# Pinning the loads, additions and stores of precomputed weight sums in their queues, and dealing the jobs out anew

## The chip, the cores and the metric

The kernel runs on one core of one Trainium2 chip. The metric is the device time of one execution in microseconds (us); the median of three runs stands for a kernel. A profile is taken of one further execution. The engines are called PE (matrix products; PEld is its weight load), DVE (elementwise work and sums), ACT (copies, activations, and the issue of stores), POOL, and SP (the issue of loads). Each works through its own queue in order.

## The reference

Two residual layers over 256 tokens of width 2048 in float32: layer 0 mixes tokens with neighbourhood attention, layer 1 with a gated short convolution; after each comes a gated MLP of width 5632 with a convolution of three taps.

```python
def reference(...):
    h = x
    for i in range(DEPTH):                       # DEPTH = 2
        a = rms_norm(h, mix_norm[i])
        if m == 0:
            mixed = neighborhood_attention(a, na_w_qkv[j], na_rpb[j], na_w_o[j])   # 16 heads of 128
        elif m == 1:
            mixed = short_conv_mixer(a, sc_w_in[j], sc_conv_w[j], sc_w_out[j])     # W_out(B * conv3(C * h))
        h = h + mixed
        h = h + conv_glu_ffn(rms_norm(h, ffn_norm[i]), ffn_w_up[i], ffn_conv_w[i], ffn_conv_b[i], ffn_w_down[i])
    return rms_norm(h, final_norm)
```

## The kernel before, in words

Each float32 factor is split into two parts, hi and lo, and a product is made of three matrix products of such parts (hi by hi, hi by lo, lo by hi). The activations are split once and stay in SBUF. The weights stream from HBM in chunks of up to 512 KB: a load into a `raw` buffer (SP, lines 140, 145, 147; 6 buffers), a copy to `hi` on ACT (L171), and `lo = raw - hi` on DVE (L172; 6 buffers of each).

The program is a list of stages, each a row of items that PE takes in turn:

- `Phase` (L259, L267): the result stands with features on the partitions. A chunk is 128 output features by 8 tiles of the inner dimension; an item is mostly two feature tiles, 4 chunks. The query and key projections (`wqk`, four phases of 8 feature tiles, called QK0 to QK3 here), the up projections (`wup`, 44 feature tiles each, UP0 to UP3) and the input of the convolution (`wsc`, 48 feature tiles, SC) are phases.
- `Values` (L660 to L662): the value projection of four heads, 8 chunks and 8 items; one stands behind each QK phase (V0 to V3). Attention of those heads runs between: after a head's key come its scores (L590 to L592) two ticks later, its probabilities (L615) four ticks later, and the mix with the values after the value products.
- `Tokens` (L454 to L456): the result stands with tokens on the partitions and is added to the residual `h` (L347). These are the output of attention (`wo`), the four down projections (`wdown`; first and third by one plan, second and fourth by another, called DOWN0 to DOWN3) and the output of the convolution (`wscout`, OUT). Each has two groups of 1024 output columns. Some pairs of inner tiles are computed with seven products instead of eight, which needs sums of weight blocks. In pairs marked S, DVE makes the sums from the raw weights on the spot (lines 180 to 184). In pairs marked D they are read from DRAM, where a job left them earlier (the tile `kept`).

A job (`make`) is one half of the sums of one D pair: two loads of 256 KB into two `act` tiles (L198, on SP), four additions of 128x256 on DVE (L204 to L207), and two stores of 256 KB issued by ACT (L211). There are 76. They are listed in the order in which the Tokens stages need them, and a table deals them out to the phases: `QK_JOBS` for QK0 to QK3, `UP_JOBS` for UP0 to UP3, `SC_JOBS` for SC. Within a phase the jobs are entered in the list of chunks from an eighth of the items on to three quarters. When a chunk is prepared, the job's loads are recorded; its additions are recorded four entries of the chunk list later, its stores seven entries later. `act` tiles (22 buffers) also hold the inputs of the Tokens stages.

What sets the order: the program records its instructions in this order, and a scheduler then places them on the engines' queues by what it takes to be ready, so that an instruction recorded later can stand ahead of one recorded earlier where neither needs the other. `tc.issue_after(x)` forbids that for one pair of instructions of the same engine: what is recorded inside it stands behind `x`. It sets no bound the other way: the instruction can still slip back. Before the change it is used for a few places (the norm factor, the residual), and not for the jobs.

## Time and profile before

| what | value |
|---|---|
| median of three runs | 2233.21 us (2231.29 to 2233.58) |
| profiled execution, its own time | 2233.43 us |
| span of the profiled execution (first to last instruction) | 2231.6 us |
| granted TensorE clock, mean | 0.996 |
| PE busy | 2194.1 us (98%) |
| DVE busy | 1836.9 us (82%) |
| ACT busy | 1298.0 us (58%) |
| DMA | 530.67 MB, mean 238 GB/s |

PE's records run over one another (the matmuls are pipelined and their ends are modelled), so the 98% don't say how close PE is to its peak. What a stage could take is seen better from the distance between equal products in a stretch without waits, and from stages of equal content against one another. The time between the end of the span and the profiled execution's own time is 1.8 us.

The stages by time (us from the start of the span), as the lines of the products change: QK0 5.6, V0 57.8, QK1 81.8, V1 135.1, QK2 162.5, V2 214.8, QK3 242.4, V3 292.8, `wo` 316.3, UP0 405.4, DOWN0 652.3, UP1 763.8, DOWN1 1008.3, SC 1132.3, OUT 1410.2, UP2 1499.4, DOWN2 1746.3, UP3 1857.9, DOWN3 2102.4.

### The profile page before, as it was taken

How to read it: one execution, taken by the hardware profiler on the slowest of the kernel's cores; microseconds unless marked ns; L12 is line 12 of the kernel's file. 1: busy time of each engine (PE TensorE's matmuls, PEld its weight loads, DVE VectorE, ACT ScalarE, POOL GpSimd, SP SyncE). 2: the span in 40 equal slices, each digit the busy share in tenths (PEclk: the TensorE clock that was granted, in tenths of full speed). 3: DMA queues.
4: the chain of work that ended last, by engine and by line, in shares of the span. 5: the costliest groups of instructions: out<-in, count | busy, mean ns of one | idle time of the engine just before them, and what ended most of it. 6: DMA issues, size and time to landing. Idle time of an engine off the chain costs nothing.

```text
span 2231.6 us, 33123 instructions
## 1 busy us (share of the span) xinstructions
PE 2194.1 (98%) x11728; PEld 1893.3 (85%) x11728; DVE 1836.9 (82%) x2960; ACT 1298.0 (58%) x1967; POOL 102.4 (5%) x143
## 2 busy tenths in 40 slices
PE   9999999999999999999999999999999999999998
PEld 8878888888888888888788888878888888888886
DVE  8787679888888788878897788798888888887887
ACT  7554555666655656566564445566666655666565
POOL 0021110000000000000000001000000000000000
PEclk9999999999999999999999999999999999999999
DMA  8688656677657877767899997776776687665585
GB/s 279 224 291 280 197 173 219 205 237 234 213 177 255 273 233 245 245 197 248 255 304 325 319 337 248 249 246 199 243 234 195 208 265 245 204 212 190 166 267 174
DMA packets 288790, 530.67 MB, mean 238 GB/s; under 512 B 19568, under 2 KB 187632, under 8 KB 288624
## 3 DMA queue, kind: packets, MB, share of 16 engines
q1 hardware_dynamic: 265360, 488.07, 67.0%
q10 hardware_dynamic: 23264, 40.49, 4.9%
q8 instruction: 92, 1.51, 0.3%
q14 instruction: 74, 0.61, 0.1%
HBM read 486.54 MB, written 41.94 MB: 237 GB/s over the span
## 4 chain that ended last, share of the span: by engine, by line
PE 80%; DMA 9%; DVE 7%; issue 2%; ACT 1%; SPq 0%; ACTq 0%; POOL 0%; DVEq 0%
PE mm L259 36%; PE mm L267 19%; PE mm L454 5%; PE mm L455 5%; PE mm L456 5%; DMA act<-in_wdown 3%; DVE lo L172 3%; DMA raw<-in_wsc 2%; PE mu L454 2%; PE mu L456 2%; PE mu L455 2%; DMA raw<-in_wdown 1%; PE mm L660 1%; PE mm L662 1%; PE mm L661 1%
## 5 line engine op out<-in xcount | busy, mean ns | idle before, releaser
L171 ACT CAST hi<-raw 128x1024 fp32r<-128x1024 f32 (+1 forms) x912 | 908.9, 1013 | 390.6 <-PE mm L456 94.2
L172 DVE TENSOR_TENSOR lo<-raw,hi 128x1024 fp32r<-128x1024 f32 (+1 forms) x852 | 1013.0, 1209 | 128.3 <-ACT hi L171 71.8
L259 PE MATMUL mm<-a,hi 128*128 128x512 f32 x4096 | 961.2, 390 | 1.6 <-DVE h L347 0.8
L259 PEld LDWEIGHTS mm<-a,hi 128*128 128x128 f32 x4096 | 759.3, 188 | 154.5 <-issue 1.2
L267 PEld LDWEIGHTS mm<-a,lo 128*128 128x128 f32 x4096 | 513.5, 191 | 19.8 <-DVE lo L172 7.6
L267 PE MATMUL mm<-a,lo 128*128 128x256 f32 x4096 | 521.3, 283 | 5.3 <-DVE lo L172 5.3
L454 PE MATMUL mm<-hi,act 128*128 128x512 f32 x656 | 256.8, 392 | 2.6 <-DVE h L347 2.5
L456 PE MATMUL mm<-hi,act 128*128 128x512 f32 x656 | 256.0, 390 | 0.0
L455 PE MATMUL mm<-lo,act 128*128 128x512 f32 x600 | 234.4, 391 | 1.3 <-DVE lo L172 1.3
L312 ACT COPY corr<-mm 128x256 f32<-128x256 f32 x256 | 93.9, 371 | 228.1 <-PE mm L267 182.3
L328 DVE SCALAR_TENSOR_TENSOR conv<-pad,pt,conv 128x256 f32<-128x256 f32 x384 | 183.7, 479 | 26.4 <-ACT conv L326 20.7
L326 ACT ACTIVATE conv<-pad,pt 128x256 f32<-128x256 f32 x176 | 105.7, 601 | 149.4 <-DVE pad L318 149.2
L454 PEld LDWEIGHTS mm<-hi,act 128*128 128x128 f32 x656 | 123.7, 189 | 29.1 <-issue 2.8
L456 PEld LDWEIGHTS mm<-hi,act 128*128 128x128 f32 x656 | 123.5, 188 | 25.8
L455 PEld LDWEIGHTS mm<-lo,act 128*128 128x128 f32 x600 | 113.3, 189 | 25.6 <-DVE lo L172 2.5
L313 DVE TENSOR_TENSOR corr<-mm,corr 128x256 f32<-128x256 f32 x256 | 106.3, 415 | 7.9 <-ACT corr L312 7.8
L292 DVE TENSOR_TENSOR act<-conv,act 128x256 fp32r<-128x256 f32 x88 | 37.4, 425 | 72.1 <-ACT act L291 71.9
L318 DVE TENSOR_TENSOR pad<-corr,rstd 128x256 f32<-128x256 f32 x176 | 73.4, 418 | 0.0
L455 PE MATMUL mu<-lo,sf 128*128 128x512 f32 x168 | 67.0, 399 | 5.8 <-DVE lo L172 5.7
L204 DVE TENSOR_TENSOR act<-act 128x256 f32<-128x256 f32 x76 | 31.4, 420 | 45.9 <-DMA act<-in_wdown 34.2
L454 PE MATMUL mu<-hi,sf 128*128 128x512 f32 x168 | 66.0, 393 | 0.3 <-ACT hi L171 0.3
L456 PE MATMUL mu<-hi,sf 128*128 128x512 f32 x168 | 66.1, 394 | 0.0
(158 smaller groups left out, 1548.5 us busy)
## 6 DMA issues: line engine op xcount, KB each, us to landing
raw<-in_wup SPq DMA_DIRECT2D x352, 512.0 KB, 5.0
raw<-in_wdown SPq DMA_DIRECT2D x144, 512.0 KB, 5.3
raw<-in_wsc SPq DMA_DIRECT2D x96, 512.0 KB, 5.9
kept<-act ACTq DMA_DIRECT2D x152, 256.0 KB, 4.8
raw<-kept SPq DMA_DIRECT2D x76, 512.0 KB, 4.9
act<-in_wdown SPq DMA_DIRECT2D x128, 256.0 KB, 6.0
raw<-in_wqk SPq DMA_DIRECT2D x56, 512.0 KB, 5.1
raw<-in_wv SPq DMA_DIRECT2D x32, 512.0 KB, 4.8
```

Of the source, the lines that this page charges most:

```text
L171: nc.scalar.copy(out=hv, in_=r)
L172: nc.vector.tensor_sub(out=lv, in0=r, in1=hv.bitcast(F32))
L259: nc.tensor.matmul(self.ps[ft], lhsT=prepped[i][0][:, o:o + P], rhs=self.src[k], start=k == 0, stop=False)
L267: nc.tensor.matmul(self.ps[ft][:, S:], lhsT=prepped[i][1][:, o:o + P], rhs=self.src[k][:, :S], start=False, stop=k == self.nk - 1)
L312: nc.scalar.copy(out=corr, in_=ps[:, S:])
L313: nc.vector.tensor_add(out=corr, in0=ps[:, :S], in1=corr)
L318: nc.vector.tensor_mul(out=dst, in0=both(ps), in1=rstd)
L326: nc.scalar.activation(c, x[:, 1:S + 1], AF.Identity, scale=w[1], bias=b)
L328: nc.vector.scalar_tensor_tensor(out=c, in0=x[:, tap:tap + S], scalar=w[tap], in1=c, op0=ALU.mult, op1=ALU.add)
L454: nc.tensor.matmul(ps, lhsT=xh, rhs=wh, start=start, stop=False)
L455: nc.tensor.matmul(ps, lhsT=xh, rhs=wl, start=False, stop=False)
L456: nc.tensor.matmul(ps, lhsT=xl, rhs=wh, start=False, stop=stop)
```

## The change

Two things change. First, each load of a job is recorded behind the newest weight load on SP, each addition behind the newest L172 on DVE, and each store behind the newest L171 on ACT; `newest` keeps these three instructions. Second, the jobs are dealt out otherwise: six of the first 16 go to V0, V1 and V2 (entered after the third and, where there are two, the fifth chunk), and SC gives 14 of its 34 to the up projections.

```diff
-QK_JOBS, UP_JOBS, SC_JOBS = (0, 8, 8, 0), (8, 8, 8, 4), 34
+QK_JOBS, V_JOBS, UP_JOBS, SC_JOBS = (0, 4, 4, 2), (2, 2, 2, 0), (10, 10, 12, 8), 20
...
-                nc.sync.dma_start(out=raw[:, :w], in_=src)
+                newest["SP"] = nc.sync.dma_start(out=raw[:, :w], in_=src)
...
-        nc.scalar.copy(out=hv, in_=r)
-        nc.vector.tensor_sub(out=lv, in0=r, in1=hv.bitcast(F32))
+        newest["ACT"] = nc.scalar.copy(out=hv, in_=r)
+        newest["DVE"] = nc.vector.tensor_sub(out=lv, in0=r, in1=hv.bitcast(F32))
...
-            nc.sync.dma_start(out=x.rearrange("p (f n) -> p f n", f=2),
-                              in_=w[f:f + 2, :, 2 * i * P:(2 * i + 2) * P].rearrange("f p n -> p f n"))
+            with tc.issue_after(newest["SP"].ins):
+                nc.sync.dma_start(out=x.rearrange("p (f n) -> p f n", f=2),
+                                  in_=w[f:f + 2, :, 2 * i * P:(2 * i + 2) * P].rearrange("f p n -> p f n"))
...
             add = nc.vector.tensor_add
-            add(out=l[:, 0], in0=l[:, 0], in1=r[:, 0])
...
+            with tc.issue_after(newest["DVE"].ins):
+                add(out=l[:, 0], in0=l[:, 0], in1=r[:, 0])
...
             for n, x in enumerate(tiles):
-                nc.scalar.dma_start(out=dst[:, n, half], in_=x)
+                with tc.issue_after(newest["ACT"].ins):
+                    nc.scalar.dma_start(out=dst[:, n, half], in_=x)
...
-        def __init__(self, g, src):
+        def __init__(self, g, src, jobs=()):
...
                 chunks.append((wv[g, :, k0 * 4 * P:(k0 + 2) * 4 * P], 8 * P, "rows"))
+                if k0 in (4, 8)[:len(jobs)]:
+                    chunks.append((*jobs[k0 // 8], "make"))
...
-        Values(g, a0)
+        Values(g, a0, take(V_JOBS[g]))
```

With all 76 jobs taken, the table before gives UP3 the last two, though it names four. The new table names 76.

What this moves, engine by engine. PE's queue holds the same products in the same order, but for a few that stand some places apart. On SP, at the end of DOWN1, before the change, the loads of five jobs of SC (`act<-in_wscout`) stand among the weight loads of DOWN1 (`raw<-in_wdown`, `raw<-kept`):

```order
L147 DMA raw<-in_wdown 128x4x256 x2
L198 DMA act<-in_wscout 128x2x256 x2
L147 DMA raw<-in_wdown 128x4x256
L198 DMA act<-in_wscout 128x2x256
L147 DMA raw<-in_wdown 128x4x128
L198 DMA act<-in_wscout 128x2x256
L145 DMA raw<-kept_8495 128x1024
L198 DMA act<-in_wscout 128x2x256 x5
L145 DMA raw<-kept_8495 128x1024
L147 DMA raw<-in_wdown 128x4x256 x2
```

In the changed kernel (whose line numbers are up to 5 higher) the end of that stretch, through to the first jobs behind it:

```order
L147 DMA raw<-in_wdown 128x4x256
L147 DMA raw<-in_wdown 128x4x128
L145 DMA raw<-kept_8769 128x1024 x2
L147 DMA raw<-in_wdown 128x4x256 x4
L140 DMA raw<-in_wsc 128x1024 x4
L199 DMA act<-in_wscout 128x2x256 x4
L140 DMA raw<-in_wsc 128x1024
L199 DMA act<-in_wscout 128x2x256 x2
```

The job loads have moved out of DOWN1; the first stand behind the fourth chunk of SC. At the head of OUT the same holds for two jobs, whose loads now stand behind the fourth and fifth chunk of UP2; and two jobs that stood in `wo` now stand at the head of UP0.

On SP in the middle of SC, before (a pair of `act<-` loads is one job):

```order
L198 DMA act<-in_wdown 128x2x256 x4
L140 DMA raw<-in_wsc 128x1024 x5
L198 DMA act<-in_wdown 128x2x256 x6
L140 DMA raw<-in_wsc 128x1024 x8
L198 DMA act<-in_wdown 128x2x256 x4
L140 DMA raw<-in_wsc 128x1024 x5
L198 DMA act<-in_wdown 128x2x256 x8
L140 DMA raw<-in_wsc 128x1024 x6
```

and now:

```order
L199 DMA act<-in_wdown 128x2x256 x4
L140 DMA raw<-in_wsc 128x1024 x7
L199 DMA act<-in_wdown 128x2x256 x4
L140 DMA raw<-in_wsc 128x1024 x5
L199 DMA act<-in_wdown 128x2x256 x4
L140 DMA raw<-in_wsc 128x1024 x7
L199 DMA act<-in_wdown 128x2x256 x2
L140 DMA raw<-in_wsc 128x1024 x5
```

The bunches of two to four jobs have become bunches of one or two, with as many chunks between them.

On DVE at the head of SC, before. `a` is the normalized input of SC, `m`, `z`, `rcol` and `conv` here are steps of the norm's factor, and the additions of a job are `act<-act`:

```order
L172 TENSOR_TENSOR lo<-raw,hi 128x1024
L300 SCALAR_TENSOR_TENSOR a<-tr,pt,a 128x256 x2
L334 TENSOR_SCALAR z<-z 128x2
L172 TENSOR_TENSOR lo<-raw,hi 128x1024
L300 SCALAR_TENSOR_TENSOR a<-tr,pt,a 128x256 x2
L172 TENSOR_TENSOR lo<-raw,hi 128x1024
L300 SCALAR_TENSOR_TENSOR a<-tr,pt,a 128x256 x2
L340 RECIPROCAL m<-m 128x2
L206 TENSOR_TENSOR act<-act 128x2x128
L341 TENSOR_TENSOR m<-m 128x2
L172 TENSOR_TENSOR lo<-raw,hi 128x1024
L300 SCALAR_TENSOR_TENSOR a<-tr,pt,a 128x256
```

and now:

```order
L206 TENSOR_TENSOR act<-act 128x2x128
L337 TENSOR_SCALAR z<-z 128x2
L207 TENSOR_TENSOR act<-act 128x2x128
L172 TENSOR_TENSOR lo<-raw,hi 128x1024
L303 SCALAR_TENSOR_TENSOR a<-tr,pt,a 128x256 x2
L208 TENSOR_TENSOR act<-act 128x2x128
L343 RECIPROCAL m<-m 128x2
L206 TENSOR_TENSOR act<-act 128x2x128
L344 TENSOR_TENSOR m<-m 128x2
L209 TENSOR_TENSOR act<-act 128x2x128
L345 SCALAR_TENSOR_TENSOR m<-m,z 128x2
L207 TENSOR_TENSOR act<-act 128x2x128
```

Eight additions of two jobs stand between the pieces of the input and of the norm's factor where one stood, and two of the L172 that stood ahead of the last piece of `a` have moved behind it.

On DVE at the border from QK1 to V1, before (`qk` and `s` are steps of a head's scores and probabilities):

```order
L605 TENSOR_SCALAR s<-s,z 128x256 x2
L292 TENSOR_TENSOR qk<-qk 128x256
L207 TENSOR_TENSOR act<-act 128x2x128 x2
L204 TENSOR_TENSOR act<-act 128x2x128
L172 TENSOR_TENSOR lo<-raw,hi 128x1024
L205 TENSOR_TENSOR act<-act 128x2x128
L172 TENSOR_TENSOR lo<-raw,hi 128x1024
L206 TENSOR_TENSOR act<-act 128x2x128
L172 TENSOR_TENSOR lo<-raw,hi 128x1024
L207 TENSOR_TENSOR act<-act 128x2x128
L313 TENSOR_TENSOR corr<-mm,corr 128x256
L292 TENSOR_TENSOR act<-tr,act 128x256
```

and now, at the same border:

```order
L172 TENSOR_TENSOR lo<-raw,hi 128x1024 x2
L606 RECIPROCAL z<-z 128x2
L295 TENSOR_TENSOR qk<-qk 128x256
L608 TENSOR_SCALAR s<-s,z 128x256 x2
L206 TENSOR_TENSOR act<-act 128x2x128
L207 TENSOR_TENSOR act<-act 128x2x128
L208 TENSOR_TENSOR act<-act 128x2x128
L209 TENSOR_TENSOR act<-act 128x2x128
L172 TENSOR_TENSOR lo<-raw,hi 128x1024 x2
L316 TENSOR_TENSOR corr<-mm,corr 128x256
L295 TENSOR_TENSOR act<-tr,act 128x256
L571 TENSOR_TENSOR qk<-corr,rstd 128x256
```

Where the additions of two jobs ran into each other and into the L172 of the value products, those of one job stand in a row; the next two jobs stand farther on, among the L172 of V1 and QK2.

More of the change, by code (lines that the diff above doesn't have):

```diff
@@ L144, in prep_to @@
             if kind == "kept":
-                nc.sync.dma_start(out=raw, in_=src().rearrange("p h n -> p (h n)"))
+                newest["SP"] = nc.sync.dma_start(out=raw, in_=src().rearrange("p h n -> p (h n)"))
             else:
-                nc.sync.dma_start(out=raw[:, :4 * w].rearrange("p (f c) -> p f c", f=4),
-                                  in_=src.rearrange("f p c -> p f c"))
+                newest["SP"] = nc.sync.dma_start(out=raw[:, :4 * w].rearrange("p (f c) -> p f c", f=4),
+                                                 in_=src.rearrange("f p c -> p f c"))
             r = raw[:, :4 * w].rearrange("p (f k c) -> p f k c", f=4, c=P)
@@ L185, in sums @@
         return w22, parts(t13), parts(r)
-    kept = {}
+    kept, newest = {}, {}
     def make(job, half):
@@ L203, in adds @@
             add = nc.vector.tensor_add
[L204 to L207 removed]
+            with tc.issue_after(newest["DVE"].ins):
+                add(out=l[:, 0], in0=l[:, 0], in1=r[:, 0])
+                add(out=r[:, 0], in0=r[:, 1], in1=r[:, 0])
+                add(out=r[:, 1], in0=l[:, 0], in1=r[:, 1])
+                add(out=l[:, 1], in0=r[:, 1], in1=l[:, 1])
         def store():
             for n, x in enumerate(tiles):
[L211 removed]
+                with tc.issue_after(newest["ACT"].ins):
+                    nc.scalar.dma_start(out=dst[:, n, half], in_=x)
         stores.append((len(prepped) + 4, adds))
```

3 lines of the change are left out of this document (removed).

## The prediction

> **What bounds the kernel now.** First the page's totals, then the chain of waits for the pace of a stretch without waits, then the busy times by stage, then the waits inside the stages that are too long.
>
> ```profile
> span 2231.6 us, 33123 instructions
> PE 2194.1 (98%) x11728; PEld 1893.3 (85%) x11728; DVE 1836.9 (82%) x2960; ACT 1298.0 (58%) x1967; POOL 102.4 (5%) x143
> 430.19 7.28 PE mm L259 x32
> 437.47 3.83 PE mm L267 x32
> ```
>
> PE is never without work for long, and the chain shows its pace: two feature tiles of a phase take 7.28 us for the long products and 3.83 for the short ones, 11.11 in all; a long product 0.23, a short one 0.12. PE's products are the floor. What can be won is the time that a stage takes beyond them. The stages (length; busy time and instructions of each engine; clock; DMA share; GB/s), in the order V0, QK1, V1, QK2, V2, QK3, V3, UP0, DOWN0, UP1, DOWN1, SC, OUT, UP3 (UP2 is as UP0 to 0.1 us):
>
> ```profile
> 57.80:81.80 24.00, 24.00 (x117) 19.93 (x115) 20.90 (x35) 12.35 (x24) 3.16 (x3) 1.00 0.72 228
> 81.80:135.10 53.30, 51.37 (x311) 45.80 (x310) 38.53 (x81) 25.07 (x45) 5.50 (x2) 1.00 0.80 270
> 135.10:162.50 27.40, 24.28 (x112) 19.55 (x111) 23.59 (x40) 15.08 (x28) 5.85 (x2) 1.00 0.82 273
> 162.50:214.80 52.30, 50.97 (x307) 45.40 (x306) 37.70 (x79) 24.63 (x43) 5.69 (x2) 1.00 0.80 273
> 214.80:242.40 27.60, 24.31 (x113) 19.57 (x112) 23.75 (x40) 15.12 (x28) 4.88 (x2) 1.00 0.83 275
> 242.40:292.80 50.40, 50.40 (x307) 45.28 (x306) 34.00 (x58) 28.36 (x49) 2.04 (x2) 1.00 0.51 163
> 292.80:316.30 23.50, 23.50 (x113) 19.59 (x112) 18.32 (x31) 11.88 (x23) 0.00 (x0) 1.00 0.56 180
> 405.40:652.30 246.90, 246.90 (x1428) 218.59 (x1427) 203.50 (x356) 153.43 (x243) 12.20 (x24) 1.00 0.67 215
> 652.30:763.80 111.50, 111.50 (x494) 92.34 (x493) 92.51 (x107) 66.80 (x74) 0.00 (x0) 1.00 0.77 251
> 763.80:1008.30 244.50, 244.50 (x1409) 216.56 (x1409) 207.32 (x355) 145.83 (x228) 12.30 (x24) 1.00 0.70 228
> 1008.30:1132.30 124.00, 117.18 (x511) 94.67 (x509) 106.47 (x139) 72.96 (x91) 0.00 (x0) 0.99 0.82 272
> 1132.30:1410.20 277.90, 272.39 (x1554) 238.94 (x1555) 223.33 (x413) 135.29 (x200) 15.62 (x16) 1.00 0.88 294
> 1410.20:1499.40 89.20, 86.28 (x378) 69.82 (x377) 79.28 (x102) 54.21 (x72) 0.00 (x0) 0.98 0.79 268
> 1857.90:2102.40 244.50, 244.50 (x1410) 216.58 (x1409) 200.48 (x331) 147.31 (x228) 12.64 (x24) 1.00 0.62 203
> ```
>
> UP1 and UP3 take 244.5 us, which is 22 x 11.11: no wait at all. Against this measure, or against a twin, four places are long. QK1 and QK2 take 2.9 and 1.9 us more than QK3, which has no job. V1 and V2 take 3.9 and 4.1 more than V3, and V0 0.5 more. Sum 13.3. DOWN1 takes 12.5 more than DOWN0, of which some 2 are the 17 more short instructions on PE (transposes); 10.5 are left. SC should take 24 x 11.11 = 266.6, and 2.4 for its start (UP0 less UP1); it takes 8.9 more. OUT has 360 products; at DOWN0's pace (111.5 us for 492) they take 81.6, with 2 for transposes 83.6, and it takes 5.6 more. Together 38 us, all in stages where jobs are loaded. UP0, UP1 and UP2 carry six to eight jobs each and lose nothing.
>
> **How a job makes PE wait.** In DOWN1 (start, length, what):
>
> ```profile
> 1084.06 4.01 SPq L198 DMA_DIRECT2D act<-in_wscout  x5
> 1090.17 0.43 DVE L204 TENSOR_TENSOR act<-act 128x256 f32<-128x256 f32 x1 [2.63 <-DMA act<-in_wscout]
> 1091.27 0.34 SPq L145 DMA_DIRECT2D raw<-kept  x1
> 1092.72 0.60 PE L455 MATMUL mu<-lo,sf 128*128 128x512 f32 x1 [3.35 <-DVE lo L172]
> 1093.12 0.63 PE L456 MATMUL mu<-hi,sf 128*128 128x512 f32 x1
> 1095.68 0.63 PE L456 MATMUL mu<-hi,sf 128*128 128x512 f32 x1
> ```
>
> Five loads of 256 KB for SC's jobs hold SP for 4 us, and only then is the second half of a kept sum loaded that PE needs next. DVE stands 2.63 us in an addition whose load has not landed, with `lo` behind it. PE waits 3.35 us, and the eight products from 1092.72 to 1095.68 start 0.40 to 0.43 us apart where 0.23 is their pace: 1.6 us more. In SC:
>
> ```profile
> 1269.61 2.98 SPq L198 DMA_DIRECT2D act<-in_wdown  x4
> 1277.60 0.43 DVE L204 TENSOR_TENSOR act<-act 128x256 f32<-128x256 f32 x1 [3.31 <-DMA act<-in_wdown]
> 1280.03 0.65 ACT L312 COPY corr<-mm 128x256 f32<-128x256 f32 x2 [2.71 <-DVE act L204]
> 1280.93 1.22 PE L267 MATMUL mm<-a,lo 128*128 128x256 f32 x8 [1.87 <-DVE lo L172]
> L204 DVE TENSOR_TENSOR act<-act x76: 412/418/428, 104.5 to 1979.7; 128x256 f32<-128x256 f32 x76
>   DMA act<-in_wdown: 34.2, 19
> ```
>
> Loads issued at 1269.6 let their addition start at 1277.6; DVE idled 3.31 us, ACT stood behind its store for 2.71, PE waited 1.87. Over the run DVE idled 34.2 us before first additions for the weights of the down projections, 19 times. At the border of V1 the same wait goes straight into the scores, and ACT stands 5.84 us behind its stores:
>
> ```profile
> 131.69 0.43 DVE L204 TENSOR_TENSOR act<-act 128x256 f32<-128x256 f32 x1 [1.62 <-DMA act<-in_wdown]
> 132.50 0.38 PE L591 MATMUL sc<-qk 128*128 128x256 f32 x1 [1.72 <-DVE qk L292]
> 136.11 0.37 ACT L312 COPY corr<-mm 128x256 f32<-128x256 f32 x1 [5.84 <-DMA kept<-act]
> ```
>
> In OUT two job loads stand ahead of the weights, and later PE waits for the residual, which DVE reaches late:
>
> ```profile
> 1414.24 2.10 SPq L198 DMA_DIRECT2D act<-in_wdown  x4
> 1455.08 0.77 PE L454 MATMUL mm<-hi,act 128*128 128x512 f32 x1 [2.45 <-DVE h L347]
> ```
>
> **The change, part by part.** No instruction is added or removed: 76 jobs, 152 loads, 304 additions, 152 stores before and after. Only places move.
>
> *DOWN1.* The ten loads and the 20 additions (20 x 0.418 = 8.4 us of DVE) of five jobs leave it, with their stores. The waits shown go. What is late next is seen in DOWN3, which runs the same plan without jobs: there PE still waits for two `lo`, 0.9 us in all.
>
> ```profile
> PE mm L455 <- DVE lo L172: 0.5, 1, 0.5
> PE mu L455 <- DVE lo L172: 0.4, 1, 0.4
> ```
>
> DOWN1 has the norm's work on DVE besides. I leave 3 of the 10.5. Gain 7.5; bounds 5 (only the 3.35 and the slow products after it go) and 9.5.
>
> *SC.* 29 jobs run inside its window now, 20 then. DVE: 223.3 - 9 x 1.68 = 208.2 of some 269 us, 77%; UP1 runs at 207.3 of 244.5, 85%, without a wait. DMA: 294 GB/s x 278 us less 9.4 MB is 72 MB, 269 GB/s; DOWN0 runs at 251 without a wait, DOWN1 at 272 with some. So DMA is the closer one. The additions still stand close behind their loads, so DVE will still idle before them, but in bunches of one or two jobs instead of up to four, and the weights have time to catch up between. I leave 1.4 of 8.9. Gain 7.5; bounds 3 (each of some eleven bunches costs half a microsecond of PE) and 8.9.
>
> *OUT.* Four loads and eight additions leave it. DVE still has the combination of seven sums ahead of the residual. I leave 1.3 of 5.6. Gain 4.3; bounds 2 and 5.5.
>
> *QK and V.* 16 jobs stay in this part; QK1 and QK2 lose four each, QK3 gets two, V0, V1 and V2 two each. QK1 and QK2 no longer run into the value products with a backlog of six jobs. But V0 has DVE busy 20.9 of 24.0 us, and two jobs are 3.4 more: 24.3. V1 with V3's work and two jobs has 18.3 + 3.4 = 21.7 of 23.5. PE gets its weights well ahead, so DVE may fall behind for a while; scores and probabilities may not. Bound from above: by V1 before, two jobs at its border cost 3.9, so six cost 12 and nothing is gained. From below: all of it goes but 1. I take half, 6.8, since the jobs now come one at a time, and two of three away from the border.
>
> *The heads of SC, UP0 and UP2.* Jobs now start four chunks into these phases, where DVE writes the last pieces of the input:
>
> ```profile
> 1142.46 4.27 PE L259 MATMUL mm<-a,hi 128*128 128x512 f32 x18
> 1145.11 0.48 DVE L300 SCALAR_TENSOR_TENSOR a<-tr,pt,a 128x256 fp32r<-128x256 f32 x1
> ```
>
> The last piece is written at 1145.6, while PE is in the products that take it. Eight additions ahead of it are 3.3 us, the two `lo` that moved behind it are 2.4 less. Cost 1 at SC, 0.5 at each of the others: 2; bounds 0 and 6 (nothing moved away, at all three).
>
> *UP0 to UP3.* Their windows hold six, eight, six and two jobs now, then 10, 10, 12 and 8: with 1.68 us of DVE for each that is 210.2 of 246.9, 210.7 of 244.5, 213.6 of 246.9, 210.6 of 244.5, at most 87%. UP1's 85% without a wait covers them; if that cover fails it is by a microsecond each. Cost 0.5; bounds 0 and 4.
>
> Sum: 7.5 + 7.5 + 4.3 + 6.8 - 2 - 0.5 = 23.6. The span becomes 2208.0; with the 1.8 us around it 2209.8, and the profiled execution stands 0.2 above the median: 2209.6.
>
> By the Trainium skill ("TensorE: Matmul & The Clock Gate", Part 1), PE's clock is halved only after an idle window of about 3.4 us. The wait in DOWN1 fits that (3.35 us, then half pace); the one in OUT was 2.45 us, and the next product is recorded with 0.77 us, so the rule's length is not a safe limit here. What the rule would change is small: without the slow products OUT's 5.6 would be all waits, and the sum stays.
>
> **The rivals.**
>
> *The waits move instead of going* (the additions stay too close behind their loads). For it: they stand one or two chunks (2.8 us of PE each) behind the load in the new order as in the old, and at 1269.6 the data took 8 us to be there. Against: UP1 has the same distance and loses nothing, since it is not short of DMA. It would keep SC at its lower bound, 3, give nothing in QK and V, 7.5 in DOWN1, 3 in OUT, and cost 2.5: 11 us, 2222.
>
> *SP stands still* (slower). A job's load needs a free `act` tile; pinned behind the newest weight load it now waits at that place, and all weights wait behind it. The place is the head of SC, where eight loads come within six chunks while DOWN1 still holds `act` tiles, and the heads of UP0 and UP2. If SP stood 10 us at each of the three, the time of three to four chunks, and the weights had no lead, 30 us would be lost and the time be 2240; from 28 us in all on it decides. Against it stands how little these loads waited in SC before:
>
> ```profile
> SPq L198 <- DMA act<-in_wdown: 2.6, 2, 1.7
> ```
>
> The Trainium skill ("DMA: Bandwidth & Descriptors", Anatomy of one DMA) has the same mechanism: a DMA's wait is made by the issuing sequencer before dispatch, not by the DMA engines, so what is queued behind it waits too. The trace agrees where loads follow one another at 1084.
>
> *It does not do what it says*: the scheduler keeps most loads where it had them. In the up projections that is so, a job every four or eight chunks as before. In DOWN1 and OUT the order shows the loads gone, so only the rest of the gains could fail: 2230 to 2233.
>
> **How the numbers follow.** Forecast 0.68, waits that move 0.19, SP 0.08, no effect 0.05. A difference under 0.2% (4.5 us) can't be told from none. The forecast and the first rival are faster; so 0.87, 0.05, 0.08. The forecast's own range: bounds at their better ends give 9.5 + 8.9 + 5.5 + 12 = 35.9, 2197.3, and not all will fall so, so 2200. The upper end takes in the first rival, 2223.
>
> **What would show it.** DOWN1 at 116 us or less with no `act<-in_wscout` loads; SC near 271; OUT near 85; V1 and V2 near 25.5; the four up projections within 1 us of 246.9 and 244.5; PE's idle time before `lo` nearly gone. Wrong would be: DVE's idle time before first additions above 34 us, PE waiting in V0 to V2 for scores or probabilities as now, SP's loads of jobs with waits of microseconds at the head of SC, or any up projection longer by 3 us.

## The result

The changed kernel takes 2205.35 us, median of four runs (2203.89 to 2206.94), beside 2233.39 us of the kernel before on the same chip: a ratio of 0.9875, 95% interval 0.9858 to 0.9892. In a later comparison it took 2204.1 (ratio 0.9872, 0.9853 to 0.9890). The forecast was 2209.6 in a range from 2200 to 2223. One run of the kernel with the pins alone, below, took 3101.5 us at a granted clock of 0.654 and is left out of its time.

The page of the changed kernel, totals and the chain that ended last by engine:

```profile
span 2202.1 us, 33145 instructions
PE 2184.6 (99%) x11728; PEld 1891.3 (86%) x11728; DVE 1835.8 (83%) x2960; ACT 1288.7 (59%) x1967; POOL 90.5 (4%) x143
PE 88%; DVE 5%; DMA 5%; issue 1%; ACT 1%; SPq 0%; DVEq 0%; ACTq 0%
```

DVE's busy time is the same to 1 us (1836.9 before), as it must be. The span is 29.5 us shorter. PE's idle time gives 20 of it (37.5 before, 17.5 now), and PE's busy time 9.5, most of it in DOWN1, SC and OUT (2.5, 2.9 and 2.7). In DOWN1 and OUT products at half pace stood behind the long waits, at a granted clock of 0.5 for 3.4 us each; in SC the clock did not fall, and no run says what its 2.9 are.

The stages by busy time, as in the prediction (length; busy time and instructions of PE, PEld, DVE, ACT and POOL; clock; DMA share; GB/s), in the order V0, QK1, V1, QK2, V2, DOWN1, SC, OUT, UP2:

```profile
57.80:81.80 24.00, 24.00 (x117) 19.93 (x116) 22.67 (x42) 12.26 (x24) 3.39 (x3) 1.00 0.87 281
81.80:132.60 50.80, 50.80 (x311) 45.65 (x310) 40.42 (x77) 28.29 (x51) 2.03 (x2) 1.00 0.76 249
132.60:156.40 23.80, 23.73 (x113) 19.53 (x112) 19.67 (x35) 9.86 (x21) 2.90 (x2) 1.00 0.80 257
156.40:206.80 50.40, 50.40 (x308) 45.28 (x307) 38.95 (x71) 28.41 (x49) 7.49 (x2) 1.00 0.79 265
206.80:231.90 25.10, 24.10 (x112) 19.42 (x111) 21.31 (x40) 10.31 (x22) 2.92 (x2) 1.00 0.79 254
997.90:1113.90 116.00, 114.73 (x510) 93.65 (x510) 101.83 (x123) 72.07 (x90) 0.00 (x0) 1.00 0.76 254
1113.90:1385.40 271.50, 269.51 (x1556) 238.33 (x1555) 211.50 (x376) 137.47 (x201) 9.61 (x16) 1.00 0.80 264
1385.40:1469.00 83.60, 83.60 (x379) 69.17 (x378) 74.33 (x92) 52.84 (x70) 0.00 (x0) 1.00 0.80 264
1469.00:1716.90 247.90, 247.41 (x1428) 218.46 (x1426) 211.60 (x382) 150.45 (x245) 11.74 (x24) 1.00 0.73 238
```

QK1, V1 and QK2 have come down to QK3's 50.4 and V3's 23.5 within half a microsecond, and OUT to the 83.6 that the prediction worked out as its floor. Against the prediction's measures V2 is still 1.6 too long, and SC and DOWN1 2.5 each. What PE still waits for, beside the end of the run and a wait at the start (what; us in all, times, longest):

```profile
PE mm L270 <- DVE lo L172: 2.0, 2, 1.1
PE mu L458 <- DVE lo L172: 1.8, 4, 0.7
PE tr L618 <- DVE s L608: 0.9, 2, 0.7
PE mm L262 <- DVE a L303: 0.5, 1, 0.5
PE st L377 <- DVE a L303: 0.5, 1, 0.5
```

`lo` was waited for 14.9 us before (5.7, 5.3, 2.6 and 1.3 in four rows of this view), and 4.3 now with a row of 0.5 that isn't shown; scores and probabilities for 7.1, and 0.9 now. But DVE's own idle time before first additions did the opposite of what the prediction named as its test:

```profile
DMA act<-in_wdown: 59.6, 33
DMA act<-in_wscout: 16.0, 5
```

It was 34.2 and 11.4. DVE stands 30 us longer in additions whose loads have not landed, and PE loses 30 us less. Nor do the stands lie where nothing is at stake: 32.8 us of them are in SC, which had 24.3 before and now loses 2.5 us instead of 8.9; 24.9 are in the up projections and the rest in QK and V. The experiments had to say why.

### The profile page after: what moved, and what is told of

The parts are those of the page before. It is cut to its first block, busy times and chain, and to the rows that moved or that the text cites. A ratio compares the mean times of both kernels' runs of the same rounds, so it can differ in the third digit from the quotient of the medians.

```text
span 2202.1 us, 33145 instructions
## 1 busy us (share of the span) xinstructions
PE 2184.6 (99%) x11728; PEld 1891.3 (86%) x11728; DVE 1835.8 (83%) x2960; ACT 1288.7 (59%) x1967; POOL 90.5 (4%) x143
## 4 chain that ended last, share of the span: by engine, by line
PE 88%; DVE 5%; DMA 5%; issue 1%; ACT 1%; SPq 0%; DVEq 0%; ACTq 0%
PE mm L262 40%; PE mm L270 21%; PE mm L458 6%; PE mm L459 6%; PE mm L457 6%; DMA act<-in_wdown 2%; DVE lo L172 2%; PE mu L458 2%; PE mu L459 2%; PE mu L457 2%; DMA raw<-in_wdown 1%; PE mm L665 1%; PE mm L667 1%; PE mm L666 1%; ACT hi L171 1%
## 5 line engine op out<-in xcount | busy, mean ns | idle before, releaser
L171 ACT CAST hi<-raw 128x1024 fp32r<-128x1024 f32 (+1 forms) x912 | 903.7, 1012 | 344.0 <-PE mm L459 91.7
L172 DVE TENSOR_TENSOR lo<-raw,hi 128x1024 fp32r<-128x1024 f32 (+1 forms) x852 | 1012.0, 1210 | 104.0 <-ACT hi L171 67.0
L458 PEld LDWEIGHTS mm<-lo,act 128*128 128x128 f32 x600 | 112.7, 188 | 24.9 <-DVE lo L172 1.9
L459 PE MATMUL mu<-hi,sf 128*128 128x512 f32 x168 | 65.4, 389 | 0.0
L457 PE MATMUL mu<-hi,sf 128*128 128x512 f32 x168 | 65.4, 389 | 0.0
```

The source lines that it names most:

```text
L171: newest["ACT"] = nc.scalar.copy(out=hv, in_=r)
L172: newest["DVE"] = nc.vector.tensor_sub(out=lv, in0=r, in1=hv.bitcast(F32))
L457: nc.tensor.matmul(ps, lhsT=xh, rhs=wh, start=start, stop=False)
L458: nc.tensor.matmul(ps, lhsT=xh, rhs=wl, start=False, stop=False)
L459: nc.tensor.matmul(ps, lhsT=xl, rhs=wh, start=False, stop=stop)
```

## The experiments

Each kernel beside the kernel before, on the same chip as that. The lengths are from the first product of a stage to the first of the next, in one profiled execution of each; the time is the median of the runs.

| kernel | QK1 | V1 | QK2 | V2 | DOWN1 | SC | OUT | time us | ratio to before |
|---|---|---|---|---|---|---|---|---|---|
| before | 53.3 | 27.4 | 52.3 | 27.6 | 124.0 | 278.0 | 89.2 | 2233.4 | |
| changed | 50.8 | 23.7 | 50.4 | 25.1 | 116.0 | 271.5 | 83.6 | 2205.4 | 0.9858-0.9892 |
| changed, again | 50.9 | 24.0 | 50.4 | 27.2 | 116.9 | 271.8 | 83.6 | 2204.1 | 0.9853-0.9890 |
| pins, old spread | 52.3 | 27.7 | 51.3 | 27.5 | 115.0 | 282.0 | 83.6 | 2226.3 | 0.9949-0.9979 |
| new spread, no pins | 50.8 | 24.4 | 50.4 | 25.1 | 122.8 | 271.2 | 89.0 | 2218.0 | 0.9916-0.9951 |
| no jobs in V | 53.0 | 27.3 | 52.2 | 27.6 | 117.2 | 272.3 | 83.6 | 2214.1 | 0.9898-0.9933 |
| loads pinned only | 50.9 | 24.1 | 50.4 | 24.6 | 117.9 | 270.8 | 83.6 | 2206.1 | 0.9862-0.9900 |
| additions later | 50.9 | 23.4 | 50.4 | 23.6 | 115.5 | 272.8 | 83.7 | 2202.6 | 0.9825-0.9883 |
| additions sooner | 50.9 | 27.6 | 50.4 | 31.7 | 116.0 | 273.4 | 83.6 | 2216.5 | 0.9887-0.9945 |
| heads later | 50.9 | 25.7 | 50.4 | 24.7 | 117.1 | 270.2 | 83.6 | 2207.2 | 0.9846-0.9903 |
| lighter SC | 50.9 | 23.5 | 50.4 | 23.7 | 118.8 | 269.4 | 83.6 | 2211.0 | 0.9863-0.9920 |
| additions on a scratch tile | 56.5 | 29.3 | 54.5 | 28.3 | 125.9 | 270.0 | 88.3 | 2241.3 | 1.0020-1.0048 |
| third spread | 50.9 | 23.7 | 50.4 | 24.6 | 115.3 | 271.7 | 83.6 | 2205.3 | 0.9853-0.9893 |
| third spread, additions later | 50.9 | 23.6 | 50.4 | 23.6 | 117.1 | 270.7 | 83.6 | 2202.0 | 0.9843-0.9874 |

One profile of a stage is worth a microsecond or two: the changed kernel's V2 was 25.1 in one execution and 27.2 in another, its DOWN1 116.0 and 116.9.

### The pins alone

```diff
-QK_JOBS, V_JOBS, UP_JOBS, SC_JOBS = (0, 4, 4, 2), (2, 2, 2, 0), (10, 10, 12, 8), 20
+QK_JOBS, V_JOBS, UP_JOBS, SC_JOBS = (0, 8, 8, 0), (0, 0, 0, 0), (8, 8, 8, 4), 34
```

> All pins kept, the jobs spread as in the kernel before: eight in QK1 and QK2, none between the value products, 8, 8, 8, 4 in the up projections, 34 planned in SC. Theory 'place' (what counts is at which chunk of which stage a job's loads stand; the pins matter only where they put loads out of a stage of tokens): DOWN1 116, OUT 83.6 as in the changed kernel; QK1, QK2, V1 and V2 as before, so nothing of the 10.4 us there; SC with 34 jobs in its window, 14 more than the changed kernel, as long as before (278) or some microseconds longer; 2218 to 2224 us. Rival 'density alone' (SC's loss goes with the number of jobs in it, 3.1 us at 20, 9.6 at 29): SC 281, 2222 to 2225. Rival 'pins' (adds and stores at their own place are the gain, the table is idle): 2205 to 2209, with QK1 to V2 at the changed kernel's lengths.

DOWN1 and OUT gain all that the whole change gains there, QK1 to V2 keep their loss to about 1 us a stage, and SC is worse than before. By stage that is "place", and SC's length is also what "density alone" gave it (281). The time of 2226.3 is above both ranges; the nine runs counted lie between 2219.8 and 2230.0, and the profiled one, whose stages these are, took 2222.8. SC's row and its commonest wait in this kernel:

```profile
1121.90:1403.90 282.00, 274.59 (x1555) 239.99 (x1554) 228.53 (x431) 135.59 (x201) 15.62 (x16) 0.99 0.90 306
PE mm L270 <- DVE lo L172: 6.2, 10, 1.8
```

What the pins push out of DOWN1 has to go somewhere. With the old spread five jobs more land in SC (34 instead of 29), which gives back 4 of the 14.5 us won (8.9 in DOWN1, 5.6 in OUT).

### The spread alone

```diff
-            with tc.issue_after(newest["SP"].ins):
-                nc.sync.dma_start(...)
+            nc.sync.dma_start(...)
...
-            with tc.issue_after(newest["DVE"].ins):
+            if True:
...
-                with tc.issue_after(newest["ACT"].ins):
+                if True:
```

> The new spread of the jobs, no pin at all. By the order of instructions four job loads go back into DOWN1, two into OUT and two into WO, and SC holds 16. Theory 'place': QK and V keep their 10 us; SC below 271.5 by up to 3, since it holds four jobs less; DOWN1 keeps its 123 to 124 and OUT its 88 to 89, since their loads are back; 2214 to 2218 us. Rival 'pins': QK and V lose their gain too, 2225 to 2232. Rival 'density alone': four jobs in DOWN1 instead of five are worth a fifth of its 8 us, and two in OUT as before, 2214 to 2216, the same as 'place' here.

"Pins" falls: QK1 to V2 are as in the changed kernel. DOWN1 and OUT lose nearly what they lost before, and 2218.0 is the upper edge of what "place" allowed. DOWN1 with four jobs instead of five gives 1.2 back, which "density alone" (1.6) fits as well, so the two are not told apart here. PE's waits in this kernel:

```profile
PE mu L457 <- DVE lo L172: 7.3, 7, 3.2
PE mu L456 <- DVE a L302: 3.4, 1, 3.4
PE mm L456 <- DVE h L349: 1.6, 1, 1.6
```

The pins alone are worth 7.1 us and the spread alone 15.4, by medians; together they are worth 28.0, which is 5.6 more than the sum (3.1 more by the spans of the profiled executions). SC alone would give 3.8 of that: it loses 4.1 with the pins alone, gains 6.7 with the spread alone, and gains 6.5 with both. With the pins it has to take the jobs that leave DOWN1, and in these runs it did so without loss only where the spread had made room. DOWN1 takes 2.2 of it back, since part of its gain comes from the spread too.

### The value products without jobs

```diff
-QK_JOBS, V_JOBS, UP_JOBS, SC_JOBS = (0, 4, 4, 2), (2, 2, 2, 0), (10, 10, 12, 8), 20
+QK_JOBS, V_JOBS, UP_JOBS, SC_JOBS = (0, 8, 8, 0), (0, 0, 0, 0), (10, 10, 12, 8), 20
```

> As the changed kernel, all pins kept, but the first sixteen jobs as before: eight each in QK1 and QK2, none between the value products. Theory 'place' (the jobs that QK1 and QK2 can't hold run into the value products): QK1 53.3, V1 27.4, QK2 52.3, V2 27.6 as before, everything behind as in the changed kernel; 2214 to 2217 us. Rival 'pins' (in QK and V too the addition and store kept in their place are the gain, at most a third is the spread): 2205 to 2209.

2214.1 us, in the range of "place"; the four stages are as before to 0.3 us, with the same waits, though every instruction is pinned:

```profile
PE sc L594 <- DVE qk L295: 3.4, 4, 1.4
PE tr L618 <- DVE s L608: 3.2, 4, 1.1
PE mm L666 <- DVE lo L172: 2.5, 2, 1.4
```

So in QK and V all of the gain is the spread: eight jobs queued in QK1 run into V1 with a backlog, four do not, and two more have room between the value products.

### The loads pinned, additions and stores free

```diff
-            with tc.issue_after(newest["DVE"].ins):
+            if True:
...
-                with tc.issue_after(newest["ACT"].ins):
+                if True:
```

> As the changed kernel, but only the loads are pinned; additions and stores are placed freely. The loads stand as in the changed kernel (18 instead of 19 in one up projection). Theory 'place' (loads alone matter): within 1.5 us of the changed kernel, 2204 to 2207. Rival 'pins': the additions slip ahead of the loads that feed them or ACT stands behind its stores, 2209 or more, with DVE's idle time before first additions above the changed kernel's 75.6 us.

2206.1 us, within 1.5 of the changed kernel, with intervals that overlap nearly wholly. Against the run without pins (2218.0) the pin on SP alone is worth 11.9 us. Of the three pins only that one does anything that can be measured; DVE's idle time before first additions is 80.3 us here (65.4 and 14.9).

### Additions later, additions sooner

```diff
-        stores.append((len(prepped) + 4, adds))
-        stores.append((len(prepped) + 7, store))
+        stores.append((len(prepped) + 7, adds))     # sooner: + 2
+        stores.append((len(prepped) + 10, store))   # sooner: + 5
```

> As the changed kernel, but a job's additions stand three chunks later behind its loads (7 instead of 4) and its stores too (10 instead of 7); the loads stay. DVE's idle time before first additions, 75.6 us in the changed kernel, should fall below 20. Theory 'lead' (DVE may stand idle in an addition as long as the split weights are some chunks ahead of PE, so this idle time costs next to nothing): 2203 to 2208 us, SC within 1 us of 271.5, the four up projections unchanged. Rival 'idle' (PE's remaining loss comes from these waits, as it did in SC and DOWN1 of the kernel before): SC 268.5 to 269.5, DOWN1 the same as it holds no jobs, 2200 to 2203. A third outcome: act tiles are held three chunks longer, SP stands before loads of jobs for a free tile, and SC grows by 2 us or more.

> As the changed kernel, but a job's additions stand two chunks sooner behind its loads (2 instead of 4) and its stores too (5 instead of 7); the loads stay. DVE's idle time before first additions should rise from 75.6 us to 150 or more. Theory 'lead': idle time costs nothing where DVE's busy and idle time together stay below the stage's length; the up projections have 30 to 40 us of room and stay within 1 us of 246.9, 244.5, 247.9, 244.5; SC has some 60 us of room for 20 jobs and loses 0 to 5 us; 2204 to 2212. Rival 'idle': every wait of DVE passes to PE in part (in the kernel before 45.6 us of idle time went with some 20 us of PE's loss in these stages, 0.4 for each), so 75 us more cost 15 us or more, 2218 and above, the up projections longer by 2 to 4 us each.

Over the whole run neither edit did to DVE's idle time what it was to do: 67.0 us with the additions later, 87.3 sooner, beside 75.6. In the up projections the additions hardly moved: in UP1 two `lo` run between a job's loads and its first addition in the changed kernel, two with the additions sooner and 2.3 on the mean with them later, and in the phases most additions still start 6 to 8 us behind their loads. So there neither was tested as meant. Between the value products the edits did move them. DVE's stands in V1 and V2 are none with the additions later, 3.1 and 2.8 us in the changed kernel, and 5.2 and 7.1 sooner; the two stages together take 47.0, 48.9 and 59.4 us, and with the additions later PE waits for nothing in them. The later kernel's 2202.6 lies in the range of "idle", but not for its reason (SC was to be 269.5 at most, and is 272.8); what it gains over the changed kernel is in V1 and V2. The sooner kernel is more telling. Its four up projections are within 0.4 us of the changed kernel's (246.7, 244.5, 247.5, 244.5) and SC loses 1.9, as "lead" said, but V1 and V2 lose 3.9 and 6.6, which neither theory had, and 2216.5 is above the range of "lead". In V2 of the sooner kernel, DVE and then PE:

```profile
227.24 0.15 DVE L606 RECIPROCAL z<-z 128x2 f32<-128x2 f32 x1
232.45 0.42 DVE L206 TENSOR_TENSOR act<-act 128x256 f32<-128x256 f32 x1 [5.06 <-DMA act<-in_wdown]
232.80 1.34 DVE L608 TENSOR_SCALAR s<-s,z 128x256 f32<-128x256 f32 x2
234.03 1.09 PE L618 MATMUL tr<-pt,s 128*128 128x128 f32 x4 [5.26 <-DVE s L608]
235.34 0.63 PE L666 MATMUL mm<-lo,a 128*128 128x512 f32 x1
```

The softmax's last step stands one place behind an addition. DVE idles 5.06 us for the load, and PE idles 5.26 us for DVE: the wait passes on whole. Elsewhere the same kind of stand passes on nothing. In SC of the changed kernel DVE stands 5.06 us too, at 1181.57 us, and PE's first wait there comes 90 us later. In UP1 DVE stands 0.8 to 2.7 us in six of ten jobs, and the stage takes its 244.5 us without a wait:

```profile
1181.57 0.42 DVE L206 TENSOR_TENSOR act<-act 128x256 f32<-128x256 f32 x1 [5.06 <-DMA act<-in_wscout]
753.40:997.90 244.50, 244.50 (x1410) 216.59 (x1409) 207.62 (x361) 142.07 (x228) 11.74 (x24) 1.00 0.72 236
```

What separates the two is not how long DVE stands but what stands behind it: weights that PE needs later than the wait lasts, or a result that PE needs at once. The 15 us of "idle" (0.4 for each) is no rate of the kernel, but a mean over both. SC says the same across the runs: with the pins alone DVE stands 24.4 us in it and it takes 282.0; with the lighter SC of a later run DVE stands 35.4 us, PE waits for no `lo`, and it takes 269.4.

### Jobs away from the heads

```diff
-            made, lo, hi = 0, len(order) // 8, len(order) * 3 // 4
+            first = sum(len(ks) == 1 and len(two) == 1 for two, ks in order)
+            made, lo, hi = 0, max(first, len(order) // 8), len(order) * 3 // 4
```

> As the changed kernel, but the first jobs of UP0, SC and UP2 wait until the feature tiles that are made one by one are over: first loads at chunks 19, 8 and 19 instead of 4; as many jobs in each stage as before. Theory 'heads' (jobs among the last pieces of the input cost 1 to 2 us at SC and UP2): the head of UP2 falls to 0.7 of loss as UP0 and UP2 had before, UP2 246.9; SC the same or 0.5 shorter; UP0 246.9; 2203 to 2205. Rival: UP2's loss at its head comes from the normalisation of another kind of run and stays at 1 to 1.7; 2205 to 2206. Rival 'density': 18 to 20 jobs in a shorter stretch of SC cost more than the head gains, SC 272 to 274.

2207.2, no measurable difference to the changed kernel. SC is 270.2, 1.3 less and better than "heads" gave it, UP2 247.8 as it was (its loss moved from 14 us behind its start to 185 us), and DOWN2, which had none, lost 1.8, with a wait of 1.0 for `corr` near its start. The rival "density" fell for SC, and "heads" for UP2. SC's 1.3 is no more than one profile differs from another.

### Fewer jobs in SC

```diff
-QK_JOBS, V_JOBS, UP_JOBS, SC_JOBS = (0, 4, 4, 2), (2, 2, 2, 0), (10, 10, 12, 8), 20
+QK_JOBS, V_JOBS, UP_JOBS, SC_JOBS = (0, 4, 4, 4), (2, 2, 0, 0), (10, 12, 12, 12), 14
```

> As the changed kernel with other numbers of jobs: 4, 4, 4 in QK1 to QK3, two each in V0 and V1 and none planned in V2, 10, 12, 12, 12 in the up projections, 14 in SC. Theory 'density' (SC's loss goes with the jobs in it: 13.6 at 34, 9.6 at 29, 3.1 at 20, 2.8 at 16): SC 270.5 to 271, little is left to gain below 16 jobs; UP1 and UP3 carry 12 and stay at 244.5; V2 gains up to 1; 2202.5 to 2205. Rival 'too many in the up projections' (12 jobs are 20 us of DVE on 194, 88% of the stage, and the additions' idle time comes on top): UP1 and UP3 longer by 1 to 3 us each, 2206 to 2210.

2211.0, the rival's side and above its range. SC falls to 269.4, 1.1 less than "density" hoped for, and V2 to 23.7; but UP1 and UP3, with 12 jobs that all start behind their first quarter, take 245.1 and 246.5, and the stages behind them 118.8 and 127.7 (the last one to PE's end), 2.8 and 4.5 more than in the changed kernel. At the border of UP1 and DOWN1, DVE and PE:

```profile
1001.67 0.42 DVE L316 TENSOR_TENSOR corr<-mm,corr 128x256 f32<-128x256 f32 x1
1002.15 0.50 PE L457 MATMUL mm<-hi,act 128*128 128x512 f32 x1 [2.33 <-DVE corr L316]
1003.30 0.63 PE L458 MATMUL mm<-lo,act 128*128 128x512 f32 x1
```

DVE ends the phase behind, and the first products of the next stage wait for a `corr` that frees their PSUM tile. UP2 bears 12 jobs, and three of them start in its first eighteen chunks. That speaks for a limit on the jobs of each stretch, not of each stage, but UP2 also has another stage behind it, and no run tells the two apart.

In the changed kernel's SC the two waits that are left stand where two jobs come at one place. Here is the second (SP, then DVE):

```profile
1295.96 1.98 SPq L199 DMA_DIRECT2D act<-in_wdown  x4
1301.75 0.43 DVE L206 TENSOR_TENSOR act<-act 128x256 f32<-128x256 f32 x1 [1.96 <-DMA act<-in_wdown]
1305.23 1.22 DVE L172 TENSOR_TENSOR lo<-raw,hi 128x1024 fp32r<-128x1024 f32 x1
```

Four loads at 1296, a stand of 1.96 us, and eight additions that start among the `lo` from 1301.8 on; PE waits 1.13 us for the `lo` of 1305.2. With 14 jobs nearly each place has one, and SC has no wait for `lo`. But two at one place is not the cause by itself: the changed kernel has six such places in SC and waits behind two, and the run with jobs away from the heads has nine and no wait for `lo` at all. What makes the difference stays open.

### Additions that wait for no load, in the kernel before

```diff
-LEAD = 96
+LEAD = 32
...
+    scratch = cp.tile([P, 2 * P], mybir.dt.bfloat16, name="scratch")
...
-            add(out=l[:, 0], in0=l[:, 0], in1=r[:, 0])
-            add(out=r[:, 0], in0=r[:, 1], in1=r[:, 0])
-            add(out=r[:, 1], in0=l[:, 0], in1=r[:, 1])
-            add(out=l[:, 1], in0=r[:, 1], in1=l[:, 1])
+            for _ in range(4):
+                add(out=scratch, in0=pt[:, :2 * P], in1=pt[:, P:3 * P])
```

> The kernel before, but the 304 additions of the jobs add constants into a small tile of their own, so that they wait for no load and the kept sums are not the sums; loads, stores and DVE's work stay, and the loads stand at the same chunks. Theory 'DVE stands' (in the kernel before, PE's loss beside jobs comes from DVE standing in an addition until its data land, with lo, corr, scores or h queued behind it): DOWN1 116 to 118, SC 270 to 272, OUT 84 to 85, V1 and V2 24 to 26, 2203 to 2212 us. Rival 'loads' (the loads themselves hold SP and the DMA engines, so weights come late whether DVE stands or not): DOWN1 121 or more, SC 276 or more, QK1 to V2 as before, 2225 or more. Between them: DOWN1 and SC each keep a third to a half.

The edit also shrinks the tile `lead`, which no instruction reads or writes, from 96 columns to 32; what that does by itself was not tried. The premise failed in part: additions that depend on nothing were hoisted, all 304 of them into the first 510 us (first and last start at the end of this row):

```profile
L206 DVE TENSOR_TENSOR scratch<-pt x304: 397/424/1290, 20.4 to 509.8; 128x256 bf16<-128x256 f32 x152
```

So the stages up to UP0, up to 3.2 us longer each than before, say nothing of the question, and nor does the time of 2241.3. From UP1 on the kernel has the job loads and stores of the kernel before, the loads within a chunk of the same places, and no additions of jobs at all. DOWN1, SC and OUT, and behind them what SP and ACT waited for from 1080 to 1130 us, in DOWN1:

```profile
1022.90:1148.70 125.80, 119.79 (x510) 95.38 (x509) 100.68 (x121) 73.21 (x91) 0.00 (x0) 0.97 0.81 272
1148.70:1418.80 270.10, 269.40 (x1556) 238.31 (x1555) 186.24 (x295) 134.37 (x200) 8.13 (x16) 1.00 0.88 301
1418.80:1507.10 88.30, 85.38 (x379) 70.16 (x378) 75.76 (x94) 54.09 (x72) 0.00 (x0) 0.98 0.79 271
```

```profile
SPq L199 <- DMA kept<-act: 10.4, 2, 6.1
ACT hi L171 <- DMA act<-in_wscout: 6.3, 3, 4.4
```

The two theories each have a stage. SC, with 29 jobs' loads and stores, falls from 278.0 to 270.0 at 301 GB/s: without the additions it is within 1.0 of the 269.0 that the prediction held it to, so the transfers cost no more than that. Whether DVE's standing or its work was the cost is not told apart, since both are gone (DVE is busy 186.2 us there instead of 223.3). DOWN1 and OUT stay at 125.9 and 88.3 without a single addition of a job. There a job's loads wait for `act` tiles that the stores of other jobs still hold, SP stands 10.4 us with the weights behind it, and ACT stands 6.3 us in stores whose data have not come, with `hi` behind them. How much is SP's part and how much ACT's was not separated, and the edit moved the waits: in DOWN1 of the kernel before SP stood 4.1 us for such stores and DVE 5.1 in additions. So the run shows that loads and stores alone can cost these stages as much, not that the additions had no part before. What removes it is that the loads no longer stand among the weights of these stages, which the pin on SP does.

Two rows of SP's waits before a job's load over the whole run of the kernel before, and then the three largest such rows of the changed kernel:

```profile
SPq L198 <- DMA act<-in_wdown: 8.1, 12, 1.7
SPq L198 <- DMA kept<-act: 6.1, 3, 3.0
```

```profile
SPq L199 <- PE mm L262: 4.8, 11, 0.9
SPq L199 <- PE mm L270: 1.6, 4, 0.6
SPq L199 <- DMA act<-in_wscout: 1.4, 2, 0.9
```

A job's load no longer waits for stores of other jobs, and no wait before one is above 0.9 us now.

### A third spread, and the changed kernel again

```diff
-QK_JOBS, V_JOBS, UP_JOBS, SC_JOBS = (0, 4, 4, 2), (2, 2, 2, 0), (10, 10, 12, 8), 20
+QK_JOBS, V_JOBS, UP_JOBS, SC_JOBS = (0, 4, 4, 4), (2, 2, 0, 0), (12, 10, 12, 10), 16
```

> As the changed kernel with another spread of the jobs: 4, 4, 4 in QK1 to QK3, two each in V0 and V1, none planned in V2, 12, 10, 12, 10 in the up projections, 16 in SC. From the runs so far: V2 23.7 as with the lighter SC (1.5 less than the changed kernel), SC 269.5 to 270.5 (1 to 2 less), UP1 and UP3 with 10 jobs stay at 244.5, UP0 with 12 as UP2 with 12 at 247 to 248 (0 to 1 more); 2200.5 to 2203.5 us, 0.1% faster than the changed kernel. Rival: 10 jobs in UP3 push work into DOWN3 as 12 did (4.5 us there) and it is 2204 to 2207.

> The same spread (4, 4, 4; two and two; 12, 10, 12, 10; 16), with additions three chunks later and stores too, as in the run with later additions. If what that run gained lay in V1 and V2 alone, the new spread already has it: within 1 us of the same spread with the additions at 4. If DVE's idle time before additions still costs PE something in SC, 1 to 2 us less.

> The changed kernel itself once more, as the measure for the two other spreads on the same chip: 2204 to 2207 us, each stage within 1.5 us of its first profile.

All on one chip: 2205.3 for the third spread, 2202.0 with the additions later too, 2204.1 for the changed kernel. The first is above its range and in its rival's, with DOWN3 1.2 us longer than in the changed kernel; the second is 3.3 below the first, more than either outcome named; the third is as expected but for V2. The middle one is the fastest by 0.1%, but the intervals of its ratio and of the changed kernel's overlap (0.9843 to 0.9874 and 0.9853 to 0.9890), so that it beats the changed kernel isn't shown; that it beats the kernel before is. UP0 with 12 jobs and UP1 and UP3 with 10 lose nothing (246.8, 244.5, 244.5). SC did not fall as hoped with 16 jobs, three times two at one place: 271.7 and 270.7, with one or two waits for `lo` of 0.7 to 1.2 us where the changed kernel has them. The changed kernel's second profile holds one wait more, in V2, which is nearly half of the 4.6 us by which its profiled executions differ:

```profile
214.98 0.72 PE L618 MATMUL tr<-pt,s 128*128 128x128 f32 x4 [1.84 <-DVE s L608]
216.57 0.63 PE L666 MATMUL mm<-lo,a 128*128 128x512 f32 x1
```

With the additions later V2 took 23.6 in both kernels that have them so, without a wait of PE in V1 or V2, where the others with additions at 4 had 0.2 to 1.8 us of waits for `s` in most profiles. That fits a gain of 1 to 3.6 us in V2; that it carries to the time isn't shown.

## Why the prediction was right, point by point

The direction and the main mechanism held: the waits sat beside job loads, and they went where the loads went or where the jobs were spread. The time was 4.3 us below the forecast, near the middle of the lower half of the range. The terms, measured between the first profiles of the two kernels, with the changed kernel's second profile in brackets:

- *DOWN1*, forecast 7.5: 7.9 (7.0). Right; pinning the loads alone gives 6.1. But the reading there leaves out a step. The five loads hold SP until 1088.1 us, and the load of the kept sum at 1091.27 then waits 3.1 us more, for a sum that stands on DVE behind the addition of 1090.17 and its stand of 2.63 us. So both the loads and DVE's stand had a part, and the runs don't say how much each (DVE, then what SP waited for):

```profile
1090.51 0.68 DVE L184 TENSOR_TENSOR raw<-raw 128x512 f32<-128x512 f32 x1
SPq L145 <- DVE raw L184: 3.1, 1, 3.1
```

- *SC*, forecast 7.5 less 1 for its head: 6.5 (6.2). Right. But "DMA is the closer one" was wrong: with no additions SC ran at 301 GB/s and lost 1.0 us.
- *OUT*, forecast 4.3: 5.6 (5.6). Nothing of the 1.3 that were left for the combination of seven sums was needed: with the jobs gone the residual is not late. It is just above the upper bound of 5.5.
- *QK and V*, forecast 6.8 as half between two bounds: 10.4 from the start of V0 to the end of V3 (8.2). This is the term that was mis-sized most. The bound at which nothing is won rested on V1 before, where two jobs cost 3.9; but they cost that as the tail of a backlog of eight, and alone between the value products they cost nothing in V0 and at most 0.5 in V1. V2 kept 1.6 to 3.7 of its loss, so here the bound was half right.
- *Heads*, forecast 1 at SC and 0.5 each at UP0 and UP2: 0 at UP0, 1.0 at UP2 (1.1), and at SC perhaps the 1.3 that it was shorter with the jobs away from the heads. The sum of 2 comes out, but not for its reason alone: UP2 kept its loss when its jobs left the head, and in the third spread it has jobs at the same places and 247.0 us.
- *UP0 to UP3*, forecast 0.5: nothing beside UP2's head. The cover named there, DVE below 87%, is real but close: 12 jobs in UP1 and UP3 broke it, for 0.7 and 2.0 in them and 2.8 and 4.5 behind them.

Of the rivals, "waits move instead of going" had its condition come true and its price not: the additions do wait as close behind their loads as before, and DVE stands 75.6 us in them instead of 45.6. The prediction took DVE's stand for PE's loss, and so named 34 us as the sign that it would be wrong; that step failed, though the forecast did not hang on it. What the runs showed in its place is that a stand costs by what is queued behind it: 5.26 us for one of 5.06 ahead of a softmax step, nothing for one of 5.06 in SC or for 10.3 us of them in UP1. "SP stands still" did not come: the job loads' longest wait on SP is 0.9 us. It was, in part, the state of the kernel before.

Alone the spread counts for more than the pins: 15.4 us against 7.1. "It does not do what it says" did not come for the loads, as DOWN1 and OUT show; of the pins on additions and stores the time shows no effect.

## What to carry to other kernels

Before counting an in-order engine's idle time as a loss, look at the first instructions queued behind it: weights that are some microseconds early absorb the stand, a softmax step or a residual passes it on whole. Background transfers belong in stages where such work is not next, and spread: here SC took 282.0 us with 34 jobs, 278.0 with 29, and 269.4 to 273.4 with 14 to 20. If one stage is cleared of them, make room where they will land, or that stage gives part of the gain back.

## What the runs showed of the hardware

A load of 256 KB among weight loads of 512 KB took 5.9 us from issue to landing (median of 128 in the changed kernel), at 240 to 300 GB/s over the stages, and that is what DVE stands for when its addition follows too soon.

Half pace behind a wait is not a matter of the wait's length alone. Before the products of a run end, the granted clock in the traces falls to 0.5 for 3.41 us at a time, or twice that, and the falls of one run lie whole multiples of that apart: in the kernel before they begin at 1092.97 and 1454.78 us, 361.81 us apart, which is 106 times 3.413. So each run can be cut into fixed windows of 3.413 us. Two rows show the changed kernel's second profile, around the wait of 1.84 us above, and three the new spread without pins, where PE waited 3.41 us in OUT, up to 1451.88 (PE's busy time and products; clock; DMA share; GB/s):

```profile
212.95:216.36 3.41, 1.57 (x12) 1.00 0.98 311
216.36:219.77 3.41, 3.41 (x10) 0.50 0.46 147
```

```profile
1446.69:1450.10 3.41, 1.78 (x8) 1.00 0.00 0
1450.10:1453.52 3.42, 1.64 (x7) 1.00 0.49 153
1453.52:1456.93 3.41, 3.41 (x16) 1.00 0.48 154
```

The shorter wait lies in one window, leaves 1.57 us of busy time in it, and the next window runs at half clock, with eight products 0.43 us apart from 216.57 on where 0.23 is their pace, some 1.5 us more. The longer wait is shared by two windows, and the clock stays. Over all the traces, without the first 20 and the last 25 us of each, the clock fell behind 13 windows, in which PE was busy for 0 to 55%. It fell behind every window with less than 47% and behind none with more than 56%; in between both occur. PE's ends are modelled, so these shares are rough.

The Trainium skill ("TensorE: Matmul & The Clock Gate", Part 1) has the clock halved after an idle window of about 3.4 us, and says that the window runs freely, so its phase varies. The fixed distances agree with that; a halving behind a window in which PE was busy for 46% does not fit a window that must be idle throughout. The measurement decides: here a wait of 1.84 us could cost some 1.5 us more and one of 3.41 us nothing, by how they fell on the windows.
